# Seven-product output projection: the in-place sums of weight tiles issued by GpSimd in place of VectorE

## The chip, the cores and the metric

The kernel runs on one core of one Trainium2 chip. The metric is the device time of one execution in microseconds; the median of several runs counts. A core has five instruction queues that run side by side, each strictly in its own order: PE (TensorE, matrix products), DVE (VectorE, elementwise), ACT (ScalarE, elementwise and copies with a change of type), POOL (GpSimd) and SP (SyncE, which here issues most DMAs). Between queues an instruction waits on semaphores that the other queue's instructions raise when they end.

## The reference

One layer of a hybrid decoder for a prompt of 512 tokens (with 16 meta tokens in front) and 8 sample tokens. A normalised input is projected to queries, keys, values, gates and the input of a state-space branch; a windowed attention branch and the state-space branch are computed; both are merged. All in float32. The change lies in the last product of the merge, with `w_out` (2048 x 2048):

```python
def merge(x, o_attn, z_a, y_ssm, z_s, g_a, g_s, w_attn_out, w_ssm_out, w_out):
    br_a = (o_attn * jax.nn.silu(z_a)) @ w_attn_out
    br_s = (y_ssm * jax.nn.silu(z_s)) @ w_ssm_out
    return x + (jax.nn.sigmoid(g_a) * br_a + jax.nn.sigmoid(g_s) * br_s) @ w_out
```

## The kernel before

**Float32 products in three parts.** TensorE multiplies in a rounded float32 format (fp32r). Each operand is therefore split into `hi` (the rounded value, made by a ScalarE copy) and `lo` (the rest, made by a VectorE subtraction), and each product is the sum of hi x hi, lo x hi and hi x lo. A weight tile of 128 x 1024 comes by DMA as `raw` and is split into `whi` and `wlo`. For most of the program the class `Stream` does this (lines L783 to L785).

**The last stage: seven products for eight.** The product with `w_out` takes the token columns in two halves and the rows and columns of the weight in 2 x 2 blocks, and replaces each 2 x 2 block product, which would need eight products, by seven products of sums (the scheme of Strassen and Winograd). The sums of the activations are made beforehand, into the tiles `cb0` to `cb7`: seven combinations each, with hi and lo parts (L1244 to L1257, in the loop over `i` from 0 to 15 that also computes the attention half of the merge with `mm`, L901). The sums of the weights are made on the fly by the class `Quads`. A quad is four raw weight tiles, and there are eight quads (the loop over `j` in steps of two, from L1271 on). For product number s of a quad, `SUMS[s]` names the raw tile that is first added to in place and the one that is added, and `SRC[s]` the raw tile that is then split:

```python
    LOADS = (0, 1, 2, None, 3, None, None)
    SUMS = (None, None, (1, 2), (1, 0), None, (2, 0), (1, 3))
    SRC = (0, 1, 1, 1, 3, 2, 1)
```

So four of seven products need a sum, 32 in the whole stage, and three of the four build on each other in the same tile (raw 1): the next sum may only overwrite the tile when the split of the one before has read it, and the split can only begin when the sum is there. `make` (L827) writes for each product the sum (L839), the copy to `whi` (L840) and the subtraction to `wlo` (L841); the load of the raw tile is L823, issued by SP. `get` keeps three further products made ahead of the one in use. There are three buffers of the raw tiles and of `whi` and `wlo` in one pool and four, and two, in another.

**The products.** `product` (L1261 to L1265) issues 24 matmuls into one PSUM bank: for each of the eight `cb` tiles p two with `whi` and one with `wlo`. Four banks (`ab` and `cd`, the tiles `mm` and `aux`) hold the four blocks of the result. Between the products ScalarE copies two of the banks out (L1293, L1295), and VectorE combines them (L1297, L1301, L1302, L1304, L1307) and adds the input `x` (L1279, in the function `out`, which then has SP write the result, L1280).

**What sets the order.** The program is written in one sequence; the tile framework's scheduler reorders it by priorities and its own cost estimates into the five queues, and inserts the semaphores. `high_priority` around `make` puts the splits and sums ahead of other work. The scheduler may also mix the matmuls of two products that go to different banks. What a queue's order is can be read from the built program.

Of the kernel before, what the change touches and what calls it, by code (L numbers as in the profile page):

```python
# [12 lines left out]
ALU = mybir.AluOpType  # L13
# [752 lines left out]
class Stream:  # L766
# [20 lines left out]
    def make(self, i):  # L787
        with self.tc.high_priority(offset=HIGH):
            self.piece(i, self.tiles(i), slice(0, 8))
# [9 lines left out]
class Quads:  # L799
# [27 lines left out]
    def make(self, r):  # L827
        nc = self.nc
        q, s = divmod(r, 7)
        if self.LOADS[s] is not None:  # L830
            self.load(4 * q + self.LOADS[s] + 4)
        t = self.raw[4 * q + self.SRC[s]]
        pool, bufs = (self.pool, 3) if r % 5 < 3 else (self.more, 2)
        hi = pool.tile([P, 8, P], F32R, name="whi", bufs=bufs)
        lo = pool.tile([P, 8, P], F32R, name="wlo", bufs=bufs)
        with self.tc.high_priority(offset=HIGH):
            if self.SUMS[s]:
                o, i = (self.raw[4 * q + j] for j in self.SUMS[s])
                nc.vector.tensor_tensor(out=o, in0=o, in1=i, op=ALU.add)  # L839
            nc.scalar.copy(out=hi, in_=t)  # L840
            nc.vector.tensor_tensor(out=lo, in0=t, in1=hi.bitcast(F32), op=ALU.subtract)  # L841
        self.parts[r] = hi, lo
# [602 lines left out]
```

## Time and profile before

| | |
|---|---|
| median of 3 runs | 1327.99 us (1327.48 to 1329.24) |
| the profiled execution's own time | 1328.25 us |
| its span, from the first instruction to the last | 1326.5 us |
| mean granted TensorE clock | 0.995 of full speed |
| ScalarE busy | 439.4 us (33%) |
| last products (L1264) | from 1146.4 us to the end of the span |
| TensorE busy in 1146.4 to 1158.5 us | 6.43 of 12.10 us |
| TensorE busy in 1207.0 to 1306.4 us | 98.77 of 99.40 us |

The profile is one execution, recorded by the hardware. A view by lines groups equal instructions: line, engine, operation, the tile written and the tiles read, count, then busy time and the mean duration, then the time in which the engine stood idle just before them, and what ended that. A timeline row has the start, the duration, the engine, the line and the tiles; in brackets stands the idle time before it and what ended it. The chain of waits runs back from the last instruction and names what ended each wait. A table of windows gives, for each stretch, the busy time of PE, PE's weight loads, DVE, ACT and POOL with the number of instructions, then the granted clock, the DMA share and GB/s. Matmuls overlap, so a single one's duration is more than what the next has to wait.

### The profile page before, as it was taken

How to read it: one execution, taken by the hardware profiler on the slowest of the kernel's cores; microseconds unless marked ns; L12 is line 12 of the kernel's file. 1: busy time of each engine (PE TensorE's matmuls, PEld its weight loads, DVE VectorE, ACT ScalarE, POOL GpSimd, SP SyncE). 2: the span in 40 equal slices, each digit the busy share in tenths (PEclk: the TensorE clock that was granted, in tenths of full speed). 3: DMA queues.
4: the chain of work that ended last, by engine and by line, in shares of the span. 5: the costliest groups of instructions: out<-in, count | busy, mean ns of one | idle time of the engine just before them, and what ended most of it. 6: DMA issues, size and time to landing. Idle time of an engine off the chain costs nothing. (4 is left out here: it accounts for less than half of the span.)

```text
span 1326.5 us, 26594 instructions
## 1 busy us (share of the span) xinstructions
PE 1304.1 (98%) x10804; PEld 1262.0 (95%) x10804; DVE 1009.3 (76%) x1914; ACT 439.4 (33%) x726; POOL 52.4 (4%) x124
## 2 busy tenths in 40 slices
PE   9999999999999999999899999999999999899997
PEld 8999999999999999999898999999999999899997
DVE  8887778787969697967668587787876377878784
ACT  8322222222223132322444343335423133433341
POOL 0000000000000000001300201000010000000000
PEclk9999999999999999999999999999999999999999
DMA  8337263635444444344864356347677665535531
GB/s 279 116 129 222 94 190 114 177 97 177 127 149 138 144 129 145 108 126 141 219 201 138 108 155 189 128 130 224 183 245 247 200 190 178 191 120 160 155 113 50
DMA packets 98267, 209.71 MB, mean 158 GB/s; under 512 B 16812, under 2 KB 39324, under 8 KB 98112
## 3 DMA queue, kind: packets, MB, share of 16 engines
q1 hardware_dynamic: 93472, 194.11, 46.5%
q0 software_dynamic: 4672, 13.89, 3.9%
q8 instruction: 85, 1.39, 0.5%
q14 instruction: 38, 0.31, 0.1%
HBM read 175.32 MB, written 34.74 MB: 158 GB/s over the span
## 5 line engine op out<-in xcount | busy, mean ns | idle before, releaser
L901 PE MATMUL mm<-xh,whi 128*128 128x260 f32 (+1 forms) x2048 | 421.3, 286 | 0.0
L901 PE MATMUL mm<-xh,wlo 128*128 128x260 f32 (+1 forms) x2048 | 417.5, 285 | 0.0
L901 PE MATMUL mm<-xl,whi 128*128 128x260 f32 (+1 forms) x2048 | 416.3, 284 | 0.0
L784 ACT CAST whi<-raw 128x1024 fp32r<-128x1024 f32 (+3 forms) x188 | 186.0, 995 | 520.0 <-PE mm L901 356.2
L901 PEld LDWEIGHTS mm<-xh,whi 128*128 128x128 f32 x2048 | 318.0, 189 | 9.7 <-issue 9.3
L901 PEld LDWEIGHTS mm<-xl,whi 128*128 128x128 f32 x2048 | 318.6, 189 | 3.9 <-issue 3.9
L901 PEld LDWEIGHTS mm<-xh,wlo 128*128 128x128 f32 x2048 | 316.2, 188 | 4.2 <-issue 4.1
L785 DVE TENSOR_TENSOR wlo<-raw,whi 128x1024 fp32r<-128x1024 f32 (+3 forms) x188 | 215.7, 1152 | 44.3 <-ACT whi L784 42.3
L901 PE MATMUL mm<-Y,whi 128*128 128x260 f32 x768 | 125.5, 284 | 0.0
L901 PEld LDWEIGHTS mm<-Y,whi 128*128 128x128 f32 x768 | 105.7, 188 | 2.3 <-issue 2.3
L1264 PE MATMUL mm<-cb,whi 128*128 128x260 f32 x512 | 93.5, 283 | 1.7 <-DVE T L1297 0.7
L840 ACT CAST whi<-raw 128x1024 fp32r<-128x1024 f32 x56 | 58.3, 1051 | 96.4 <-PE mm L1264 45.6
L901 PE MATMUL mm<-A,whi 128*128 128x260 f32 x512 | 82.2, 282 | 0.0
L1264 PEld LDWEIGHTS mm<-cb,whi 128*128 128x128 f32 x512 | 78.8, 188 | 2.3 <-DVE T L1297 0.9
L1264 PE MATMUL aux<-cb,whi 128*128 128x260 f32 x384 | 73.9, 291 | 7.1 <-DVE cb L1257 2.9
L841 DVE TENSOR_TENSOR wlo<-raw,whi 128x1024 fp32r<-128x1024 f32 x56 | 68.2, 1223 | 16.4 <-ACT whi L840 13.6
L901 PE MATMUL mm<-Y,wlo 128*128 128x260 f32 x384 | 77.6, 283 | 0.0
L1264 PE MATMUL mm<-cb,wlo 128*128 128x260 f32 x256 | 72.1, 283 | 0.6 <-DVE wlo L841 0.6
L901 PEld LDWEIGHTS mm<-A,whi 128*128 128x128 f32 x512 | 70.2, 188 | 0.0
L1264 PEld LDWEIGHTS aux<-cb,whi 128*128 128x128 f32 x384 | 62.0, 196 | 7.8 <-DVE cb L1257 3.2
L928 DVE TENSOR_TENSOR z<-mm,R 128x520 f32<-128x520 f32 x43 | 30.0, 697 | 45.0 <-PE mm L901 43.8
L901 PEld LDWEIGHTS mm<-Y,wlo 128*128 128x128 f32 x384 | 59.3, 188 | 0.4 <-issue 0.4
(384 smaller groups left out, 1689.8 us busy)
## 6 DMA issues: line engine op xcount, KB each, us to landing
raw<-in_w SPq DMA_DIRECT2D x202, 512.0 KB, 3.8
gD<-z SPq DMA_DIRECT2D x48, 260.0 KB, 2.2
t<-gD SPq DMA_DIRECT2D x32, 260.0 KB, 2.7
cache<-in_kc POOLq DMA_DIRECT2D x15, 288.0 KB, 3.4
cache<-in_vc POOLq DMA_DIRECT2D x15, 288.0 KB, 3.5
xr<-in_x SPq DMA_DIRECT2D x16, 268.0 KB, 6.3
sD<-z SPq DMA_DIRECT2D x16, 260.0 KB, 2.1
z<-sD SPq DMA_DIRECT2D x16, 260.0 KB, 3.0
```

The source lines that it names most:

```text
L784: nc.scalar.copy(out=hi, in_=raw)
L785: self.dve = nc.vector.tensor_tensor(out=lo, in0=raw, in1=hi.bitcast(F32), op=ALU.subtract).ins
L840: nc.scalar.copy(out=hi, in_=t)
L841: nc.vector.tensor_tensor(out=lo, in0=t, in1=hi.bitcast(F32), op=ALU.subtract)
L901: m = nc.tensor.matmul(ps[:, c, 0:W], lhsT=wt[:, k], rhs=xo(kt, c), start=f, stop=l)
L928: v.tensor_tensor(out=z, in0=ps, in1=R_[:, :, 8:CH], op=ALU.mult)
L1264: nc.tensor.matmul(bank, lhsT=wt[:, p], rhs=cb[p][:, e, x], start=first and f and p == 0, stop=l and p == 7, skip_group_check=not first an ...
```

## The change

One word changes: the engine that is given the in-place sums.

```diff
             if self.SUMS[s]:
                 o, i = (self.raw[4 * q + j] for j in self.SUMS[s])
-                nc.vector.tensor_tensor(out=o, in0=o, in1=i, op=ALU.add)
+                nc.gpsimd.tensor_tensor(out=o, in0=o, in1=i, op=ALU.add)
             nc.scalar.copy(out=hi, in_=t)
             nc.vector.tensor_tensor(out=lo, in0=t, in1=hi.bitcast(F32), op=ALU.subtract)
```

What is computed stays the same. The scheduler orders the last stage anew.

VectorE, from the last activation sums of the stage before (`T0`, `T1` are their pieces, `cb7` the last tile of activations) to the end of `cb7`. Before:

```order
L1245 TENSOR_TENSOR T0_13938<-z_13994,t_13992 128x520
L839 TENSOR_TENSOR raw_13939<-raw_13939,raw_13866 128x1024
L1252 TENSOR_TENSOR T1_14055<-T0_13938 128x2x260
L1256 TENSOR_TENSOR cb7_14053<-T0_13938,cb7_14053 128x780
L1253 SCALAR_TENSOR_TENSOR T1_14055<-T1_14055,T0_13938 128x260
L841 TENSOR_TENSOR wlo_14091<-raw_13939,whi_14090 128x1024
L1254 TENSOR_TENSOR T1_14055<-T1_14055,T0_13938 128x260
L841 TENSOR_TENSOR wlo_14098<-raw_14075,whi_14097 128x1024
L839 TENSOR_TENSOR raw_13939<-raw_13939,raw_14075 128x1024
L841 TENSOR_TENSOR wlo_14151<-raw_13996,whi_14150 128x1024
L1257 TENSOR_TENSOR cb7_14053<-T1_14055,cb7_14053 128x1040
```

VectorE in the same place now:

```order
L1245 TENSOR_TENSOR T0_13938<-z_13994,t_13992 128x520
L1252 TENSOR_TENSOR T1_14055<-T0_13938 128x2x260
L841 TENSOR_TENSOR wlo_14086<-raw_13939,whi_14085 128x1024
L1253 SCALAR_TENSOR_TENSOR T1_14055<-T1_14055,T0_13938 128x260
L1256 TENSOR_TENSOR cb7_14053<-T0_13938,cb7_14053 128x780
L1254 TENSOR_TENSOR T1_14055<-T1_14055,T0_13938 128x260
L1257 TENSOR_TENSOR cb7_14053<-T1_14055,cb7_14053 128x1040
```

All four sums of the first quad (two of them stood just above the first rows shown) have left the queue, and three splits that stood ahead of L1257 now stand behind it.

GpSimd, at the end of its queue, where there was nothing behind the DMAs of L1154:

```order
L1154 DMA zr_12515<-gD_73 128x520
L839 ISA
L839 TENSOR_TENSOR raw_13939<-raw_13939,raw_13996 128x1024
L839 TENSOR_TENSOR raw_13996<-raw_13996,raw_13866 128x1024
L839 TENSOR_TENSOR raw_13939<-raw_13939,raw_13866 128x1024
L839 TENSOR_TENSOR raw_13939<-raw_13939,raw_14075 128x1024
L839 TENSOR_TENSOR raw_14083<-raw_14083,raw_14095 128x1024
```

The ISA row loads the library that the additions need; it waits for no semaphore. The 32 sums follow, four to a quad; the second of each quad waits only for the first, the third and fourth wait for a split on VectorE.

ScalarE, where the first quad's last copies meet the second quad's first (raw_13939 is the tile of the first quad's sums, raw_14077 and raw_14083 the first two tiles of the second quad), now:

```order
L1255 CAST cb7_14053<-T1_14055 128x1040
L840 CAST whi_14150<-raw_13996 128x1024
L840 CAST whi_14090<-raw_13939 128x1024
L840 CAST whi_14097<-raw_14075 128x1024
L1293 COPY T1_14074<-mm_14072 128x260
L840 CAST whi_14180<-raw_13939 128x1024
L840 CAST whi_14212<-raw_14077 128x1024
L1295 COPY T1_14074<-aux_14073 128x260
L840 CAST whi_14244<-raw_14083 128x1024
```

L1255 has moved up from behind the three copies that follow it here, and whi_14150 from behind the other two; the rest stands as before. The copies whi_14150, whi_14090 and whi_14180 now wait for GpSimd where they waited for VectorE, and whi_14212, the first tile of the second quad, stands behind whi_14180.

## The prediction

> **What bounds the kernel now.** I read the page first, then the groups of the last stage (from 1100 us), then the chain of waits, then the timelines of VectorE and TensorE where that stage begins.
>
> ```profile
> PE 1304.1 (98%) x10804; PEld 1262.0 (95%) x10804; DVE 1009.3 (76%) x1914; ACT 439.4 (33%) x726; POOL 52.4 (4%) x124
> ```
>
> TensorE is busy 98% of the span: nothing can be won but the waits of TensorE, and a GpSimd that is idle says nothing by itself. The sums stand in the last stage alone:
>
> ```profile
> L841 DVE TENSOR_TENSOR wlo<-raw,whi 128x1024 fp32r<-128x1024 f32 x56 | 68.2, 1223 | 16.4 <-ACT whi L840 13.6 <-PE mm L1264 1.5
> L840 ACT CAST whi<-raw 128x1024 fp32r<-128x1024 f32 x56 | 58.3, 1051 | 96.4 <-PE mm L1264 45.6 <-DVE raw L839 21.2 <-PE aux L1264 20.5
> L1264 PE MATMUL mm<-cb,wlo 128*128 128x260 f32 x256 | 72.1, 283 | 0.6 <-DVE wlo L841 0.6
> L839 DVE TENSOR_TENSOR raw<-raw 128x1024 f32<-128x1024 f32 x32 | 39.1, 1221 | 0.6
> L1279 DVE SCALAR_TENSOR_TENSOR z<-T,t 128x260 f32<-128x260 f32 x24 | 10.2, 426 | 0.3
> L1302 DVE TENSOR_TENSOR T<-T 128x260 f32<-128x260 f32 x8 | 3.4, 428 | 0.2
> ```
>
> 32 sums of 1.22 us are 39.1 us of VectorE. But in the products TensorE waited for a split 0.6 us in all (third row). From the chain of waits, the pace and the start:
>
> ```profile
> 1158.47 4.86 PE aux L1264 x26
> 1163.33 8.62 PE mm L1264 x72
> 1171.95 2.87 PE aux L1264 x24
> ```
>
> A product is 24 matmuls, 2.87 us or 0.12 each; a quad (7 products) is 7 x 2.87 = 20.1 us. The first 26 took 4.86 instead of 3.11. What TensorE waits for is only at the stage's start:
>
> ```profile
> 1152.10 0.39 PE L1264 MATMUL mm<-cb,whi 128*128 128x260 f32 x1 [0.39 <-DVE cb L1256]
> 1152.32 0.28 PE L1264 MATMUL mm<-cb,wlo 128*128 128x260 f32 x1
> 1155.00 0.58 PE L1264 MATMUL aux<-cb,whi 128*128 128x260 f32 x1 [2.40 <-ACT cb L1255]
> 1158.47 0.59 PE L1264 MATMUL aux<-cb,whi 128*128 128x260 f32 x1 [2.88 <-DVE cb L1257]
> ```
>
> It lacks the last moving operand, cb7, 5.7 us in three waits, while VectorE is full with weight tiles:
>
> ```profile
> 1143.32 1.22 DVE L841 TENSOR_TENSOR wlo<-raw,whi 128x1024 fp32r<-128x1024 f32 x1
> 1144.57 2.49 DVE L839 TENSOR_TENSOR raw<-raw 128x1024 f32<-128x1024 f32 x2
> 1146.97 0.69 DVE L1244 SCALAR_TENSOR_TENSOR t<-t,mm 128x520 f32<-128x520 f32 x1
> ...
> 1148.72 0.70 DVE L1245 TENSOR_TENSOR T<-z,t 128x520 f32<-128x520 f32 x1
> 1149.33 1.22 DVE L839 TENSOR_TENSOR raw<-raw 128x1024 f32<-128x1024 f32 x1
> 1150.46 0.70 DVE L1252 TENSOR_TENSOR T<-T 128x520 f32<-128x520 f32 x1
> 1151.07 0.97 DVE L1256 TENSOR_TENSOR cb<-T,cb 128x780 fp32r<-128x780 f32 x1
> 1151.95 0.43 DVE L1253 SCALAR_TENSOR_TENSOR T<-T,T 128x260 f32<-128x260 f32 x1
> ...
> 1154.90 1.22 DVE L839 TENSOR_TENSOR raw<-raw 128x1024 f32<-128x1024 f32 x1
> 1156.04 1.22 DVE L841 TENSOR_TENSOR wlo<-raw,whi 128x1024 fp32r<-128x1024 f32 x1
> 1157.17 1.24 DVE L1257 TENSOR_TENSOR cb<-T,cb 128x1040 fp32r<-128x1040 f32 x1
> ```
>
> Four sums stand ahead of L1257, the row TensorE waits for. That is where moving them can gain. The idle time also costs clock; the columns here are the stretch, its length, the busy times, the granted clock, the DMA share and GB/s:
>
> ```profile
> 1155.00:1158.40 3.40, 0.58 (x1) 0.29 (x1) 3.40 (x3) 0.00 (x0) 0.00 (x0) 0.50 0.72 257
> 1160.00:1162.00 2.00, 2.00 (x12) 2.00 (x12) 1.23 (x1) 0.14 (x1) 0.00 (x0) 0.56 0.39 154
> 1306.00:1309.00 3.00, 2.41 (x21) 2.20 (x19) 2.35 (x4) 1.05 (x1) 0.00 (x0) 1.00 0.16 46
> 1309.00:1312.50 3.50, 3.16 (x24) 2.95 (x24) 0.25 (x2) 0.00 (x0) 0.00 (x0) 1.00 0.31 75
> ```
>
> After the stall of some 6 us the clock is 0.50 to 0.56 for a while (4.86 - 3.11 = 1.75 us); after the wait of about 2 us near 1308 it stays 1.00.
>
> **The price of one sum on GpSimd.** No row shows an addition there. The nearest:
>
> ```profile
> L430 POOL MEMSET pm<- 64x512 f32 x1 | 0.5, 526 | 0.0
> L430 POOL MEMSET Vm<- 64x256 f32 x1 | 0.3, 313 | 0.1
> ```
>
> (526 - 313) / 256 = 0.83 ns an element and 0.1 us around it, for one stream that is written. At 1024 elements that is 0.95 us for one stream (the lower bound), 1.80 for two one after the other, 2.66 for the three that a sum has, two read and one written (the upper bound). I take the middle of two and three, 2.23. The Trainium skill (GPSIMD Engine Reference, section 3.1 Elementwise) gives 4497 ns for such an addition at 2048 elements, against 2293 on VectorE; halved, 2.25 as an estimate, and the sum below would stay as it is.
>
> **Do the two engines meet?** A split L841 reads two tiles in SBUF, raw and whi, and so does each sum. No row has GpSimd reading SBUF while VectorE works. Bounds: they don't disturb each other at all, or they take turns, each waiting for the other's whole instruction. I take the second, first come first served, for the forecast: it asks nothing of memory that the rows do not show VectorE doing alone. The Trainium skill (SBUF — State Buffer, Who interferes with whom) says that a VectorE instruction with two SBUF inputs and a GpSimd instruction that reads SBUF exclude each other for a whole instruction. By that rule the sum is the forecast, without it the first rival; no run here shows it yet. What turns would take in a quad: 7 splits (8.6) + 4 sums (8.9) + L1302 and three L1279 with both inputs in SBUF (4 x 0.43 = 1.7) = 19.2 of 20.1 us. They just fit; beyond (20.1 - 10.3) / 4 = 2.45 us a sum they no longer do.
>
> **The change part by part.** Each row is laid in its new order: it starts when its engine is free, its inputs are there and it has its turn.
>
> Start. The first sum runs 1144.5 to 1146.8 on GpSimd, the second (it waits only for GpSimd's own first) to 1149.0. L1244 reads PSUM and runs meanwhile; L1245 (both inputs in SBUF) gets its turn at 1149.0, before 1148.72. L1252 to 1150.4, the split of the first sum to 1151.55, L1253; the third sum, asked for at 1151.55, holds L1256 until 1154.1 (before 1151.07). L1254 to 1155.4, ScalarE's cast L1255
>
> ```profile
> 1153.89 1.06 ACT L1255 CAST cb<-T 128x1040 fp32r<-128x1040 f32 x1 [0.27 <-DVE T L1254]
> ```
>
> to 1156.5, L1257 to 1157.8 instead of 1158.4: **-0.6 us**, out of the 4.6 that the four sums took here.
>
> First joint. Behind L1257 run three splits to 1161.2, then the fourth sum to 1163.4. ScalarE's copy of it is queued in front of the copy of the next quad's first tile: 1164.5, 1165.5; that tile's split ends 1166.9, behind one other. TensorE, resuming at 1157.8 with the slow 26 (4.86) and 24 more, is there at 1165.5 and needs the split 0.24 us later: a wait of **+1.2**. At full clock it would come 1.75 earlier and wait that much longer; the end is the same.
>
> Later joints. Laid on by the same rule, the last sum of quad 3 runs 1202.3 to 1204.5; three copies follow it, the third (quad 4's first tile) is ready at 1207.5, its split at 1209.1, TensorE was there at 1207.6: 1.5 us. The other places give 0.5, 0.7, 0.5 and 0.2; together 3.4 in place of the 0.6 above: **+2.8**.
>
> Changing hands. A row released by another engine starts 0.02 to 0.04 us later:
>
> ```profile
> 1244.88 0.02 issue
> 1244.91 1.06 ACT whi L840
> ...
> 1247.23 0.04 issue
> ```
>
> Some 34 rows would wait for a turn; 34 x 0.04 = 1.4, half of it on the path: **+0.6**.
>
> At no cost: GpSimd's last work before the sums is this group of DMA issues,
>
> ```profile
> L1154 POOL DMA_DIRECT2D zr<-gD x8: 536/536/578, 991.5 to 1008.3; - x8
> ```
>
> and the library load (the ISA row) that stands behind it waits for nothing, so over 130 us cover it; uncovered it would be a wait of its own length before the first sum. The Trainium skill (GPSIMD Engine Reference, section 2.1 Instruction dispatch) puts such a load at about 6 us; no run here shows it. The raw loads are now freed by GpSimd:
>
> ```profile
> raw<-in_w SPq DMA_DIRECT2D x29, 512.0 KB, 4.2
> ```
>
> 4.2 us to land, and in the stage no wait of ScalarE or VectorE ends on a DMA; a sum that ends 1 to 3 us later stays inside that lead (uncovered: as much again). The waits that fall away on VectorE, 39.1 us of sums, were hidden under TensorE already except for the start.
>
> Sum: -0.6 + 1.2 + 2.8 + 0.6 = +4.0. Against the profiled execution's 1328.25 that is 1332.3; this run lies 0.26 over the median of the three, so **1332.0**.
>
> **The rivals.**
> - **No meeting: faster.** Then L1245 runs at 1147.2, L1257 ends at 1153.8: -4.6, and a stall of under 2 us leaves the clock alone (as near 1308): -1.7. TensorE then reaches the first joint before GpSimd's fourth sum (1156.0 to 1158.2) has been copied, and waits 1.8; the later joints give back 0.3. -4.8: 1323.2. With the shortest sum, 0.95, 1.3 less: 1322. For it: VectorE's four sums are plainly in front of L1257. Against it: sums and splits read the same raw tiles, and while both run, two engines bring two streams each out of one memory.
> - **Saturated turns: much slower.** From 2.45 us a sum on, turns take more than a quad has. At 2.66 it is 8.6 + 10.6 + 1.7 = 20.9: 0.8 x 8 = 6.6, on top of the forecast's 4.0, and each of the seven joints is 0.4 later: 2.8. +13: 1341. For it: three streams at the memset's pace are 2.66. Against it: the pace is of writing.
> - **Part meeting, no change:** if a meeting only slows both, half-way between 1323.2 and 1332.0 is 1327.6.
>
> **How the numbers follow.** Turns with sums up to 2.45: 0.55, because it needs only that the two reads meet, and the price lies in the middle of its bounds; own range 1328 to 1337. No meeting 0.25, saturated 0.15, part 0.05. A measurement here tells 0.2% (2.7 us) from no change: 1325.3 and 1330.7. The forecast's case (bounds 1.80 us a sum, about 1328.5, to 2.45, about 1336) is slower in 7 of 10 and the same in 3; no meeting is faster in 9 of 10. Faster 0.23; same 0.55 x 0.3 + 0.03 + 0.05 = 0.24; slower 0.53. The range reaches over the rival below and to the saturated one above: 1322.5 to 1342.
>
> **What would show it.** L839 on POOL with a mean near 2.2 us, or longer where it holds the time in which it waits for its turn; L841 with rows far over its mean of 1.22 us or gaps before it without a releaser: turns. L841 still at 1.22 beside running sums: the first rival. TensorE's wait before L1257 near 5 us, and new waits for whi L840 and wlo L841 at the joints of the quads near 1165 and 1207: the steps. The forecast is wrong if L1257 ends before 1155, or if a sum is under 1.5 or over 2.5 us.

## The result, and the profile after

The changed kernel takes 1331.91 us (median of 6 runs, 1328.61 to 1332.84) against 1327.33 us before in the same session (6 runs, 1326.03 to 1329.24): ratio 1.0032, 95% interval 1.0019 to 1.0045. It is slower by 0.3%, some 4 us. The profiled execution has a span of 1330.7 us, 4.2 more than before.

The busy times of the page, after:

```profile
PE 1306.7 (98%) x10804; PEld 1263.7 (95%) x10804; DVE 998.6 (75%) x1882; ACT 438.1 (33%) x726; POOL 134.8 (10%) x156
```

VectorE gave away 32 sums of 39.1 us, but is busy only 10.7 us less (1009.3 to 998.6), and GpSimd has 82.4 us more. Where the rest went stands in the groups of the last stage (from 1100 us):

```profile
L839 POOL TENSOR_TENSOR raw<-raw 128x1024 f32<-128x1024 f32 x32 | 82.4, 2576 | 217.7 <-DMA t<-in_x 135.7 <-DVE wlo L841 68.1 <-DMA raw<-in_w 7.3
L841 DVE TENSOR_TENSOR wlo<-raw,whi 128x1024 fp32r<-128x1024 f32 x56 | 81.4, 1472 | 14.0 <-ACT whi L840 13.6 <-PE aux L1264 0.3
L840 ACT CAST whi<-raw 128x1024 fp32r<-128x1024 f32 x56 | 57.3, 1049 | 96.4 <-POOL raw L839 50.1 <-PE mm L1264 26.6 <-PE aux L1264 13.6
L1279 DVE SCALAR_TENSOR_TENSOR z<-T,t 128x260 f32<-128x260 f32 x24 | 16.9, 705 | 0.4
L1302 DVE TENSOR_TENSOR T<-T 128x260 f32<-128x260 f32 x8 | 6.3, 782 | 0.2
L1279 DVE SCALAR_TENSOR_TENSOR z<-mm,t 128x260 f32<-128x260 f32 x8 | 3.4, 426 | 17.4 <-PE mm L1264 17.4
L1304 DVE TENSOR_TENSOR T<-aux,T 128x260 f32<-128x260 f32 x8 | 3.4, 421 | 0.0
```

The splits L841 take 81.4 us instead of 68.2, and the small rows with both inputs in SBUF (L1279 from T and t, L1302) 705 and 782 ns instead of 426 and 428. The rows with one input in PSUM (mm, aux) stay at 0.42 us. A mean of 1472 ns hides two kinds of rows. The view by source gives the shortest, the median and the longest in ns:

```profile
L839 POOL TENSOR_TENSOR raw<-raw x32: 2388/2418/3427, 1145.3 to 1307.2; 128x1024 f32<-128x1024 f32 x32
L841 DVE TENSOR_TENSOR wlo<-raw,whi x56: 1210/1219/3443, 1137.1 to 1313.8; 128x1024 fp32r<-128x1024 f32 x56
```

Half of the splits or more have the old length, and the longest take nearly three times as long. One of these, in VectorE's timeline:

```profile
1180.74 0.42 DVE L1302 TENSOR_TENSOR T<-T 128x260 f32<-128x260 f32 x1
1181.08 3.44 DVE L841 TENSOR_TENSOR wlo<-raw,whi 128x1024 fp32r<-128x1024 f32 x1
```

and beside it, in GpSimd's:

```profile
1180.90 2.53 POOL L839 TENSOR_TENSOR raw<-raw 128x1024 f32<-128x1024 f32 x1 [2.67 <-DVE wlo L841]
```

The sum ends at 1183.43. The split ends 1.09 us later, at 1184.52: nearly its whole work of 1.22 us comes after the sum. This is the rule in this trace: all ten splits that begin inside a sum end 1.08 or 1.09 us after it, and the 14 sums that begin inside a row of VectorE's with both inputs in SBUF end 2.24 to 2.28 us after that row, where an undisturbed sum takes 2.39. The time in which an engine waits for its turn thus stands **inside the duration** of its row, with no releaser and no gap.

The start of the stage in VectorE's timeline, in GpSimd's, and then the waits in TensorE's, at the start and at two joints of quads (where the products of one quad pass into those of the next):

```profile
1147.24 0.69 DVE L1244 SCALAR_TENSOR_TENSOR t<-t,mm 128x520 f32<-128x520 f32 x1 [2.05 <-PE mm L901]
1147.97 2.73 DVE L1245 TENSOR_TENSOR T<-z,t 128x520 f32<-128x520 f32 x1
...
1152.83 3.11 DVE L1256 TENSOR_TENSOR cb<-T,cb 128x780 fp32r<-128x780 f32 x1
1155.86 0.42 DVE L1254 TENSOR_TENSOR T<-T,T 128x260 f32<-128x260 f32 x1
1157.40 1.24 DVE L1257 TENSOR_TENSOR cb<-T,cb 128x1040 fp32r<-128x1040 f32 x1 [1.12 <-ACT cb L1255]
```

```profile
1145.28 4.86 POOL L839 TENSOR_TENSOR raw<-raw 128x1024 f32<-128x1024 f32 x2 [135.67 <-DMA t<-in_x]
1152.65 2.46 POOL L839 TENSOR_TENSOR raw<-raw 128x1024 f32<-128x1024 f32 x1 [2.51 <-DVE wlo L841]
```

```profile
1155.99 0.39 PE L1264 MATMUL mm<-cb,whi 128*128 128x260 f32 x1 [3.62 <-DVE cb L1256]
1157.42 0.59 PE L1264 MATMUL aux<-cb,whi 128*128 128x260 f32 x1 [0.87 <-ACT cb L1255]
1158.69 0.58 PE L1264 MATMUL aux<-cb,whi 128*128 128x260 f32 x1 [0.69 <-DVE cb L1257]
...
1167.82 0.39 PE L1264 MATMUL mm<-cb,wlo 128*128 128x260 f32 x1 [0.66 <-DVE wlo L841]
...
1210.28 0.39 PE L1264 MATMUL mm<-cb,wlo 128*128 128x260 f32 x1 [1.13 <-DVE wlo L841]
```

L1245 lasts 2.73 us instead of 0.70 beside the first two sums, L1256 3.11 instead of 0.97 beside the third. The stall of the start is 5.2 us, was 5.7. New waits for splits stand at 1167.8 and 1210.3.

Where the 4.2 us of span lie can be read from TensorE's timeline by counting the stage's 1344 matmuls (56 products of 24, the first being number 0) and comparing the start of the same number in both kernels, in us:

| stretch | before | after | difference |
|---|---|---|---|
| start of matmul 0 | 1146.39 | 1147.04 | +0.65 |
| 0 to 50, the stall | 13.11 | 12.68 | -0.43 |
| 50 to 100, to behind the first joint | 7.02 | 8.44 | +1.42 |
| 100 to 1176, the later quads | 130.21 | 132.54 | +2.33 |
| 1176 to 1320, the last quad to its last wait | 21.07 | 21.52 | +0.45 |
| the last product, and what follows | 8.7 | 8.5 | -0.2 |

The first row can't be put down to the change: matmul 0 starts anywhere from 1144.53 to 1147.04 in the kernels of this document, although their queues have one and the same order up to 12 us before it.

### The profile page after: what moved, and what is told of

Read it like the earlier page. It is cut to its first block, busy times and chain, and to the rows that moved or that the text cites. A ratio compares the mean times of both kernels' runs of the same rounds, so it can differ in the third digit from the quotient of the medians.

```text
span 1330.7 us, 26607 instructions
## 1 busy us (share of the span) xinstructions
PE 1306.7 (98%) x10804; PEld 1263.7 (95%) x10804; DVE 998.6 (75%) x1882; ACT 438.1 (33%) x726; POOL 134.8 (10%) x156
## 4 chain that ended last, share of the span: by engine, by line
PE 81%; issue 6%; POOL 5%; DMA 3%; DVE 2%; ACT 1%; SPq 1%; POOLq 0%; DVEq 0%; ACTq 0%
PE mm L901 71%; POOL raw L839 5%; PE aux L591 2%; DMA sw<-rawD 1%; PE mm L988 1%; DMA raw<-in_w 1%; PE mm L1264 1%; PE aux L537 1%; PE aux L345 1%; PE aux L346 1%; PE aux L538 1%; PE aux L1065 1%; PE mm L1186 1%; PE aux L1264 1%; PE aux L392 1%
## 5 line engine op out<-in xcount | busy, mean ns | idle before, releaser
L839 POOL TENSOR_TENSOR raw<-raw 128x1024 f32<-128x1024 f32 x32 | 82.4, 2576 | 217.7 <-DMA t<-in_x 135.7
L841 DVE TENSOR_TENSOR wlo<-raw,whi 128x1024 fp32r<-128x1024 f32 x56 | 81.4, 1472 | 14.0 <-ACT whi L840 13.6
L840 ACT CAST whi<-raw 128x1024 fp32r<-128x1024 f32 x56 | 57.3, 1049 | 96.4 <-POOL raw L839 50.1
```

The lines of the kernel that those rows point to most:

```text
L839: nc.gpsimd.tensor_tensor(out=o, in0=o, in1=i, op=ALU.add)
```

## The experiments

The theory: a sum on GpSimd and a VectorE instruction with two inputs in SBUF take turns for whole instructions; this eats what the start would gain and makes splits late at the joints. Rival A: any work of GpSimd's holds VectorE up. Rival B: nothing is held up; a sum of 2.4 us and the new order are the loss.

The time of a single execution also holds 1.5 us that have nothing to do with the edits: the last product, behind a wait of some 1.8 us, took 4.67 us at a granted clock of 0.64 in some executions and 3.16 at 1.00 in others. So the kernels are also compared by the stretch from matmul 0 to matmul 1320, where that product begins: 171.4 us before, 175.2 after.

**GpSimd writes only.** In these first diffs the line taken out is that of the changed kernel.

```diff
-                nc.gpsimd.tensor_tensor(out=o, in0=o, in1=i, op=ALU.add)
+                for n in range(2): nc.gpsimd.memset(o, 0.5 + n / 4)
```

> Each sum is replaced by two fills of the same raw tile on GpSimd, so all 32 additions are left out and GpSimd only writes. Queues, waits and buffers stay. By the pace of the old memsets (0.95 us at 1024 elements) the pair takes 1.9 us, near the 2.4 us of a sum. Theory (a reading sum and a VectorE instruction with two inputs in SBUF take turns): no row of L841 over 1.25 us, L1279 and L1302 at 0.43, TensorE's wait before L1257 down to about 2 us, time 1321 to 1324. Rival A (GpSimd's work of any kind holds VectorE up, writing too): L841 again with a mean of 1.4 us or more and rows over 2.5 us, time 1327 or more. Rival B (nothing is held up, the loss comes from the length of the sum and the new order): L841 at 1.22 us as by the theory, and the time like that of the changed kernel less what 0.5 us a sum brings, 1328 to 1331.

1323.38 us; 167.2 us to the last product. By source:

```profile
L839 POOL MEMSET raw<- x64: 945/953/963, 1138.0 to 1297.3; 128x1024 f32 x64
L841 DVE TENSOR_TENSOR wlo<-raw,whi x56: 1215/1224/1227, 1136.8 to 1301.7; 128x1024 fp32r<-128x1024 f32 x56
```

No split is longer than 1.227 us and no fill longer than 0.963, although GpSimd is busy 60.7 us in the stage. Rival A falls. TensorE's waits before L1257 are 0.65 + 0.89 = 1.5 us. The half of rival B that blames the new order falls too, for the joints behind matmul 100: up to matmul 1077 TensorE (but for one matmul) and ScalarE have the changed kernel's order here, VectorE's differs in three places, and between matmul 100 and 1077 TensorE does not wait at all, where the changed kernel's waits add up to 1.74 us. The other half, the length of a sum, stays possible: a pair of fills takes 1.97 us and not 2.42, and a fill does not wait for the tile that a sum adds, so that the first one starts at 1138.0 us and not at 1145.3. The time is close to that of the prediction's first rival (1323.2), but 1.5 us of it are the last product, which ran at full clock here.

**Half a sum, and a sum twice.**

```diff
-                nc.gpsimd.tensor_tensor(out=o, in0=o, in1=i, op=ALU.add)
+                nc.gpsimd.tensor_tensor(out=o[:, 0:4], in0=o[:, 0:4], in1=i[:, 0:4], op=ALU.add)
```

> Each sum adds the first 512 of 1024 columns only; the other half of the addition is left out. Price: if it is proportional to the columns, 1.2 us at the least; if 0.3 us of the 2.4 are fixed, 1.35. Theory: the longest rows of L841 fall from 3.44 to about 1.22 + 1.3 = 2.5 us, its mean from 1.47 to about 1.35; turns of a quad take 8.6 + 4 x 1.3 + 1.7 = 15.5 of 20.1 us, so the later joints lose under 1 us and the time is 1325 to 1328.5. Rival B (no turns): L841 at 1.22, time 1322 to 1324.5.

1326.81 us; 171.5 us to the last product. A half sum takes 1.29 us (median), the longest split 2.32. From 1.29 at 512 and 2.42 at 1024 columns: 2.2 ns a column and 0.16 us fixed. The stall is as long as before (2.60 + 2.94 us in its two main waits): L1256 lasts 2.05 beside a sum, and in this run's order three splits (4.56 us, one of them beside a sum) stand ahead of L1257 again. The later quads lose 0.3 us.

```diff
-                nc.gpsimd.tensor_tensor(out=o, in0=o, in1=i, op=ALU.add)
+                for n in range(2): nc.gpsimd.tensor_tensor(out=o, in0=o, in1=i, op=ALU.add)
```

> Each sum is made twice in a row on GpSimd (the second raw tile is added two times, so the weights differ from the reference's). Theory: turns of a quad take 8.6 + 8 x 2.4 + 1.7 = 29.5 us where TensorE needs 20.1, so seven to eight quads lose 9.4 us each and more at the joints: 1395 to 1410, and the rows of L841 get a mean over 2 us. Rival B (no turns): GpSimd's 8 x 2.4 = 19.2 us still fit into a quad's 20.1, only the chain of sum, copy and split on one raw tile gets longer by 2.4 us at three places of a quad: 1345 to 1360, L841 at 1.22 us.

1403.94 us, inside the theory's range and 44 us over rival B's. The groups:

```profile
L839 POOL TENSOR_TENSOR raw<-raw 128x1024 f32<-128x1024 f32 x64 | 172.3, 2699 | 202.6 <-DMA t<-in_x 135.6 <-DVE wlo L841 61.8 <-issue 3.0
L841 DVE TENSOR_TENSOR wlo<-raw,whi 128x1024 fp32r<-128x1024 f32 x56 | 94.1, 1706 | 30.1 <-ACT whi L840 29.7
L1279 DVE SCALAR_TENSOR_TENSOR z<-T,t 128x260 f32<-128x260 f32 x24 | 33.5, 1397 | 0.8
L1302 DVE TENSOR_TENSOR T<-T 128x260 f32<-128x260 f32 x8 | 17.0, 2125 | 0.2
```

From matmul 168 to 1176 a quad takes (1362.27 - 1181.36) / 6 = 30.2 us; turns were put at 29.5, TensorE alone needs 20.1. The mean of L841 is 1.7 us, not over 2: most of the waiting fell on the small rows L1302 and L1279, 2.1 and 1.4 us instead of 0.43. The turns are the bound here, and rival B alone cannot make this time.

**GpSimd reads one stream.**

```diff
-                nc.gpsimd.tensor_tensor(out=o, in0=o, in1=i, op=ALU.add)
+                nc.gpsimd.tensor_scalar(out=o, in0=o, scalar1=1.25, scalar2=None, op0=ALU.mult)
```

> Each sum is replaced by a multiplication of the raw tile with a constant, in place: GpSimd reads one stream and writes one; the second tile of the addition is left out. Theory, in the form that one reading stream is enough to shut the other engine out: rows of L841 up to 1.22 us plus the length of the new GpSimd row, L1279 mean over 0.5 us. Rival (only two streams read on both sides meet): no row of L841 over 1.25 us, time 1321 to 1324. The price of the row also tells what the second stream costs: 1.0 to 1.9 us where streams cost one after the other, 2.4 where the second is free.

1323.53 us; 169.6 us to the last product, in another order of products (TensorE waits five times for L1297 between quads, 0.5 to 0.6 us each), so that the time says little. Neither expectation holds. The view by source, then one meeting in the timelines of GpSimd and of VectorE:

```profile
L839 POOL TENSOR_SCALAR raw<-raw x32: 2770/2779/3786, 1135.8 to 1300.2; 128x1024 f32<-128x1024 f32 x32
L841 DVE TENSOR_TENSOR wlo<-raw,whi x56: 1206/1226/2061, 1135.0 to 1305.7; 128x1024 fp32r<-128x1024 f32 x56
```

```profile
1214.31 2.88 POOL L839 TENSOR_SCALAR raw<-raw 128x1024 f32<-128x1024 f32 x1 [3.56 <-DVE wlo L841]
```

```profile
1214.90 1.64 DVE L841 TENSOR_TENSOR wlo<-raw,whi 128x1024 fp32r<-128x1024 f32 x1
```

The split begins 0.6 us into the multiplication, takes 0.4 us longer than alone and ends 0.65 us before it. Another meeting, with two small rows of VectorE's:

```profile
1191.01 2.77 POOL L839 TENSOR_SCALAR raw<-raw 128x1024 f32<-128x1024 f32 x1 [2.42 <-DVE wlo L841]
```

```profile
1191.68 0.65 DVE L1302 TENSOR_TENSOR T<-T 128x260 f32<-128x260 f32 x1
1192.37 0.43 DVE L1279 SCALAR_TENSOR_TENSOR z<-T,t 128x260 f32<-128x260 f32 x1
```

The row that begins 0.67 us into the multiplication is held up, the one that begins 1.36 us into it is not. All 13 splits that a multiplication held up end 0.65 or 0.66 us before its end, whenever they began; the eight that begin in its last 1.7 us take 1.21 to 1.23 us. A split that is let go has 1.09 us left, so it is let go 1.75 us before the end: one read stream of GpSimd's shuts VectorE's two inputs out as well, but only until about 1.0 us into an instruction of 2.77.

**Fills of a sum's length.**

```diff
-                nc.gpsimd.tensor_tensor(out=o, in0=o, in1=i, op=ALU.add)
+                for n in (8, 4, 4, 4): nc.gpsimd.memset(o[:, 0:n], 0.5 + n / 16)
```

> As the run with two fills, but one fill of 1024 and three of 512 columns for each sum, 0.95 + 3 x 0.53 = 2.5 us: the place of a sum is taken as long as by a sum (2.42 us), all 32 additions are left out, and GpSimd only writes. The scheduler's order of the stage differs from that of the changed kernel in places. From the first product of the stage to its last wait the kernel before takes 171.4 us, the changed one 175.2. Theory (the loss behind the start comes from the turns): no row of L841 over 1.25 us, 167 to 169.5 us, waits for splits at the joints under 0.6 us each. Rival B (a sum of 2.4 us makes the joints late by its length alone): L841 at 1.22 us too, but 171.5 us or more, with waits for splits of about 1 us at joints of the quads.

1325.26 us; 169.2 us to the last product, in the theory's range; no split over 1.228 us. But the range is met by the start alone: to matmul 100 this run takes 14.2 us (before 20.1), and from there to matmul 1176 it takes 134.0 us, more than the changed kernel's 132.5 and the 130.2 of before, without a single turn. TensorE's waits add up to 2.4 us in that stretch. Some are for L1297; the longest for ScalarE's copies, at three joints, are 0.44, 0.77 and 0.30 us. By the rows of those copies the first of the three goes back to a fill (four of them take 2.71 us), the other two to TensorE's own matmuls. So this run does not show that the loss of the later joints comes from turns: late fills and another order of the products cost as much here. How large the share of a sum's length is in the changed kernel's own order it can't tell.

**Where the loss lies: the first quad alone, and all but the first quad.**

```diff
-                nc.gpsimd.tensor_tensor(out=o, in0=o, in1=i, op=ALU.add)
+                (nc.vector if q else nc.gpsimd).tensor_tensor(out=o, in0=o, in1=i, op=ALU.add)
```

> Only the four sums of the first quad are on GpSimd, the other 28 on VectorE. Theory (the start of the stage wins 0.4 us and costs 0.6 us of clock, the first joint loses 0.9, the later joints lose 2.9 and only because of the later quads' sums): the start and the first joint as in the changed kernel, the later joints as before; 1331.9 - 2.9 = 1329.0, between 1328.3 and 1329.8. TensorE's waits before L1257 5.2 us. Rival (the later loss has its root in the start, whose delay is passed on from quad to quad): 1331 or more. Rival (the lone gain of the start shows once the later quads are out of the way): under 1326.

1328.34 us (11 runs, 1325.70 to 1330.02) against 1327.93 before in that session (22 runs): ratio 1.0002 (0.9993 to 1.0010), in the theory's range, but by the times no different from before. To matmul 100 it takes 21.1 us as the changed kernel does (before 20.1), from there to 1176 130.2, as before.

```diff
-                nc.gpsimd.tensor_tensor(out=o, in0=o, in1=i, op=ALU.add)
+                (nc.gpsimd if q else nc.vector).tensor_tensor(out=o, in0=o, in1=i, op=ALU.add)
```

> The four sums of the first quad stay on VectorE, the other 28 are on GpSimd. Theory: the start as before, the later joints as in the changed kernel: 1327.3 + 2.9 = 1330.2, between 1329.4 and 1331. Rival (the later loss is passed on from the start): 1327.3 to 1328.

1330.06 us (11 runs, 1329.23 to 1331.39): ratio 1.0019 (1.0010 to 1.0028). From matmul 100 to 1176 it takes 132.6 us, as the changed kernel does. The start has the order of before and its waits, within 0.2 us (0.38, 2.40 and 3.08). So the later loss is not passed on from the start. By matmul 1320 the two lose 0.96 and 3.25 us (0.4 of this ahead of matmul 100), together 4.2; the changed kernel 3.8. The first quad's own loss of 0.96 us is seen in one trace only; by the medians the two lose 0.4 and 2.1 us, less than the changed kernel's 4.6, within intervals of 1 to 2 us each way.

**A better order on VectorE alone.** Before's sums, but the first quad's work from its fourth product on is put behind the last activation sum:

```diff
-        with self.tc.high_priority(offset=HIGH):
+        with self.tc.high_priority(offset=HIGH), self.tc.issue_after(self.after) if 2 < r < 7 else ExitStack():
             if self.SUMS[s]:
...
-            v.tensor_tensor(out=T1[:, 3], in0=T1[:, 1], in1=T0[:, 1], op=ALU.add)
+            qs.after = v.tensor_tensor(out=T1[:, 3], in0=T1[:, 1], in1=T0[:, 1], op=ALU.add).ins
```

> All sums stay on VectorE; the first quad's sums, copies and splits from its fourth product on are issued only behind the last activation sum (L1254), so that fewer of them stand ahead of L1257. Theory (what the start costs is the place of the weight tiles ahead of L1257 in VectorE's queue, and the clock that the stall of 6 us takes with it): L1257 ends some 3.5 us earlier, the stall falls from 5.7 to about 3 us, the granted clock behind it stays over 0.9, and up to 1.8 us come back at the first joint, where the splits are late: 1323 to 1325.5. Rival (VectorE is full between the start and the first joint, so every us won at the start comes back there): 1326.5 to 1328.

1322.62 us (5 runs, 1322.35 to 1324.35): ratio to before 0.9965 (0.9952 to 0.9977), faster than both kernels. VectorE's timeline, and TensorE's waits:

```profile
1150.37 0.43 DVE L1254 TENSOR_TENSOR T<-T,T 128x260 f32<-128x260 f32 x1
1150.71 2.35 DVE L839 TENSOR_TENSOR raw<-raw 128x1024 f32<-128x1024 f32 x2
1152.98 1.24 DVE L1257 TENSOR_TENSOR cb<-T,cb 128x1040 fp32r<-128x1040 f32 x1
1154.14 3.49 DVE L841 TENSOR_TENSOR wlo<-raw,whi 128x1024 fp32r<-128x1024 f32 x3
```

```profile
1151.94 0.39 PE L1264 MATMUL aux<-cb,whi 128*128 128x260 f32 x1 [0.64 <-ACT cb L1255]
1154.28 0.39 PE L1264 MATMUL aux<-cb,whi 128*128 128x260 f32 x1 [1.95 <-DVE cb L1257]
```

Counted from matmul 0, L1257 ends 8.5 us on, was 12.0; the stall is 2.6 us, was 5.7; to matmul 100 3.2 us are won, and none comes back later. The time lies 0.4 us under the expected range. Of the expectation two points fail: the first joint takes nothing back, and the clock falls all the same, to 0.50 from 1156 to 1158 us.

```diff
-            if self.SUMS[s]:
-                o, i = (self.raw[4 * q + j] for j in self.SUMS[s])
+            for ab in ((1, 2), (2, 0)) if r == 2 else (self.SUMS[s],) if self.SUMS[s] and r != 5 else ():
+                o, i = (self.raw[4 * q + j] for j in ab)
```

> As in the run before it in this list, and the first quad's third sum in the order of its products (raw 2 plus raw 0, which waits for no split) is written directly behind its first, so that VectorE makes it in the idle time before L1244. Theory: one 1.22 us instruction less behind L1254, L1257 0.7 us earlier and the first joint too: 0.5 to 0.9 us below that run, 1322.5 to 1325. Rival (the first joint sets the time and does not feel it): as that run.

1323.73 us (6 runs, 1321.96 to 1324.01): ratio 0.9967 (0.9955 to 0.9979). The intervals of the two overlap; by the times the extra edit brings nothing that can be told. In its profile the stretch to matmul 100 is 0.7 us shorter than in the run before.

## Why the prediction was right, and where its terms were off

The forecast, 1332.0 us, came true (1331.91), and its mechanism, turns, is what the traces show. That the two agree to 0.1 us is luck. The forecast was +4.0 us on a median of 1327.99; measured are +4.6 against the session's 1327.33, and 4.2 to 4.3 between the two traces. There the start and the joints, forecast at +3.4, make +3.8; the +0.6 for changing hands does not exist, and a stage that began 0.65 us later stands in its place.

- **What bounds.** Right. Only waits of TensorE counted: GpSimd's 82 us and VectorE's 10.7 us less show nowhere by themselves.
- **The price of a sum**, 2.23 us, was too low: 2.42 (median; shortest 2.39), inside the bounds, near the break-even of 2.45. The estimate from the Trainium skill (GPSIMD Engine Reference, section 3.1 Elementwise), 2.25, is short by as much.
- **The engines meet.** Shown: ten splits of ten that end 1.08 or 1.09 us after the sum they began in, unchanged rows beside fills, 30.2 us a quad with doubled sums. The rule of the Trainium skill (SBUF — State Buffer, Who interferes with whom), turns for a whole instruction where GpSimd reads and VectorE has two inputs in SBUF, agrees for sums, and so does its exception for writes.
- **Start**, forecast -0.6, measured -0.43, through the steps forecast: L1245 at its turn, L1256 behind the third sum.
- **First joint**, forecast +1.2, measured +1.42, by the steps forecast: the fourth sum (1161.04 to 1164.29, held up by a split), two copies behind it, and the split of the next quad's first tile, which ends at 1167.76 and for which TensorE waits 0.66 us. TensorE came there late itself, by the windows of the 4 us behind the stall, before and after (the columns are those of the prediction's):

```profile
1158.47:1162.47 4.00, 4.00 (x21) 4.00 (x22) 1.23 (x1) 1.43 (x2) 0.00 (x0) 0.59 0.56 166
```

```profile
1158.69:1162.69 4.00, 4.00 (x18) 4.00 (x19) 3.35 (x3) 1.90 (x3) 1.65 (x1) 0.50 0.41 131
```

  In these 4 us 21 matmuls ran at a clock of 0.59, and now 18 at 0.50. This adds nothing to the joint, as the prediction reasoned: a faster TensorE would have waited longer for the same split. Nor is it shown to be the change's: in the run with all sums but the first quad's on GpSimd, whose stall is that of before, the same 4 us also held 18 matmuls; there no wait at the joint hides it, and it costs 0.4 us.
- **Later joints**, forecast +2.8, measured 2.33 + 0.45 = +2.8. In the first of the two stretches TensorE's waits add up to 1.74 us, before 0.63; each costs about 0.25 us more than its own length until the matmuls are back at their pace, and there are more of them. The greatest was forecast at 1.5 us near 1207.6, and is 1.13 at 1210.3. Its chain, in the timelines of GpSimd, VectorE and ScalarE:

```profile
1190.95 5.02 POOL L839 TENSOR_TENSOR raw<-raw 128x1024 f32<-128x1024 f32 x2 [7.52 <-DVE wlo L841]
1197.13 3.31 POOL L839 TENSOR_TENSOR raw<-raw 128x1024 f32<-128x1024 f32 x1 [1.16 <-DVE wlo L841]
1203.21 2.40 POOL L839 TENSOR_TENSOR raw<-raw 128x1024 f32<-128x1024 f32 x1 [2.77 <-DVE wlo L841]
```

```profile
1194.58 3.61 DVE L841 TENSOR_TENSOR wlo<-raw,whi 128x1024 fp32r<-128x1024 f32 x2 [2.57 <-ACT whi L840]
1198.56 2.17 DVE L1302 TENSOR_TENSOR T<-T 128x260 f32<-128x260 f32 x1
1201.92 1.22 DVE L841 TENSOR_TENSOR wlo<-raw,whi 128x1024 fp32r<-128x1024 f32 x1
1206.72 3.50 DVE L841 TENSOR_TENSOR wlo<-raw,whi 128x1024 fp32r<-128x1024 f32 x3 [0.82 <-ACT whi L840]
```

```profile
1205.64 2.94 ACT L840 CAST whi<-raw 128x1024 fp32r<-128x1024 f32 x3 [4.12 <-PE aux L1264]
```

  Two splits in a row took 3.61 us where two alone take 2.35, the next sum 3.31 instead of 2.42: 1.3 and 0.9 us of turns in one chain of sum, split, sum. The last sum ends at 1205.61, and as forecast three copies and three splits follow it up to TensorE's wait. (The row of the copies names TensorE: a matmul of its ended within 0.02 us of the sum, and the trace can't tell which of the two the first copy needed.) Three sums in that chain are also 1.2 us each longer than VectorE's. Without either TensorE would not have waited 1.13 us here by this reading, which is argued and not shown. The new order alone is not the cause, as the run with two fills shows; how the loss of all the joints divides between turns and length stays open, since the fills of a sum's length lost as much without turns, in another order.
- **Changing hands**, forecast +0.6: this term fails. A split that waited ends 1.09 us after the sum, less than its own 1.22. There is no price for the hand-over in the rows. What makes up the sum in its place, the later start of the stage (+0.65), has nothing to do with it.
- **The signs named beforehand.** L1257 ends at 1158.6, not before 1155, a sum is under 2.5 us; the waits for splits near 1165 and 1207 came at 1167.8 and 1210.3; the split rows are far over 1.22 us. Waits of TensorE's for copies (whi L840), which were named too, did not come: its matmuls show none in the stage. ScalarE's copies wait 50.1 us for sums, before 21.2.
- **At no cost**: the library load left no trace on the path. The first sum starts at 1145.28, 0.1 us behind the split that it waits for (its row names a DMA that landed at the same moment). Raw loads: one wait of 7.3 us of GpSimd's ended on one, and no wait of TensorE's behind it.
- **The rivals.** The first, 1323.2 us without a meeting, is close to what the fills gave (1323.38, with a last product at full clock). One premise of it was wrong: that a stall of under 2 us leaves the clock alone. The wait near 1308 that it was read from is 0.71 us, not about 2; behind the 1.78 us at 1317.8 of the same profile the clock was 0.64, and behind waits of 0.65 and 0.89 us the fills' kernel too lost about 1.5 us at half clock. The saturated case is what doubled sums give.

## What to carry to other kernels

Before work is moved from VectorE to GpSimd, count what VectorE reads meanwhile: a row with two inputs in SBUF that meets a sum waits until the sum has ended. Of the 39.1 us that VectorE gave away here 28.4 came back so, and the wait is to be found in the longest rows of a group, not in gaps. If only a few of the moved instructions are in the way, it is cheaper to move them in VectorE's own queue: two lines that put weight tiles behind the activations that TensorE waits for won 0.35% here, where the other engine lost 0.32%.

## What the hardware showed that was not expected

- An in-place multiplication by a constant on GpSimd takes longer (2.77 us for 1024 columns) than an addition of two tiles (2.39 to 2.42), although it reads half as much; and it shuts VectorE's two inputs out only for about its first 1.0 us, the addition for its whole length (longest split 2.06 against 3.44 us). The Trainium skill's rule of whole instructions (SBUF — State Buffer, Who interferes with whom) does not hold for this one; why wasn't tried.
- The same small wait may or may not cost clock. Behind 1.78 us of wait the last product ran at 0.64 before and after, and behind an equal 1.78 at 1.00 in the run with all sums but the first quad's on GpSimd, by the windows of the last product in these two kernels:

```profile
1317.80:1322.50 4.70, 4.67 (x24) 4.46 (x24) 0.41 (x1) 0.00 (x0) 0.00 (x0) 0.64 0.17 57
```

```profile
1320.20:1323.40 3.20, 3.16 (x24) 2.95 (x24) 0.42 (x1) 0.00 (x0) 0.00 (x0) 1.00 0.24 83
```

That is 1.5 us between executions, a third of the effect that was to be measured here. What decides it is not shown.
